# Epilogues of the projections and of the recurrence in more steps, and two evictions on another engine

## The chip, the core and the metric

The kernel runs on one core of a Trainium2 chip. The metric is the device time of one execution in microseconds, from the first to the last instruction and what lies around them. TensorE (PE) does the matmuls, VectorE (DVE), ScalarE (ACT) and GpSimd (POOL) the elementwise work and the copies out of PSUM (evictions), and all large transfers here are queued by SyncE (SP). Each engine takes its own instructions strictly in their order: an instruction that waits holds up all that stand behind it on that engine.

## What is computed

Two blocks of a network over 1024 tokens of width 1024, in fp32 and close to fp32. The first block has an even layer (pooling and a short convolution) and an odd layer, in which the change lies. The odd layer, cut to what matters:

```python
uc, rc, kc, vc, zcc, p1c, p2c, zdc = jnp.split(hc @ in_o[j], 8, axis=-1)      # 256 context tokens
yc_rwkv, ctx_states = rwkv_branch(uc, rc, kc, vc, *rp, None)
u, r, k, v, zc, p1, p2, zd = jnp.split(h @ in_o[j], 8, axis=-1)               # 1024 tokens
y_rwkv, _ = rwkv_branch(u, r, k, v, *rp, ctx_states)
y = odd_merge(y_rwkv, zc, p1, p2, zd, *cp, grid=True)
x = x + gt * y
def rwkv_branch(...):
    r = token_shift_mix(r, mu[0])        # likewise k and v
    g = jax.nn.sigmoid(ugt @ g1) @ g2
    kk = heads(k * k_k); kk = kk / jnp.maximum(jnp.sqrt(jnp.sum(kk * kk, axis=-1, keepdims=True)), 1e-12)
    for d in range(2):                   # two directions; decay, a and k_d come from w1, w2, a1, a2
        s_fin, o = wkv_scan(r_h, heads(decay), k_d, v_h, -kk, kk * a_h, init, reverse=(d == 1))
    o = outs[0] + outs[1]                # normalised per head, times lnx_g, plus lnx_b
    bonus = jnp.sum(r_h * (k_dirs[0] + k_dirs[1]) * r_k, axis=-1, keepdims=True) * v_h
    y = (o + bonus.reshape(b, l, D_BRANCH)) * g
def odd_merge(...):
    y_d = conformer_branch(p1, p2, dw_w, dw_b, ln_g, ln_b, "cols")   # convolution, layernorm, silu
    return jnp.concatenate([y_c * jax.nn.silu(z_c), y_d * jax.nn.silu(z_d)], axis=-1) @ w_out
```

`wkv_scan` is the recurrence: per head a 64x64 state that is decayed, updated and read at each token. The second block (feed-forward, a mixer with sparse attention, feed-forward) is not touched by the change.

## The kernel before

The odd layer is `layer1`. It computes the recurrence in chunks of 64 tokens, four chunks to a group and 40 groups in all: four quarters `i` of the 512 channels, two directions, five groups (one of the context, four of the tokens). A group passes `s1` (decays, the chunk's own products, written to DRAM), `elim` (the triangular inverse on VectorE and GpSimd, once for five groups) and `s2`, which runs nine groups behind `s1`: it makes the local solution KV (evicted on L765), applies the inverse with one set of matmuls whose results go to the two tiles `z[1]` and `z[0]` (evicted on L775, one on ScalarE and one on VectorE), then Q, C, and the states `SI` chunk by chunk.

Beside the recurrence run *dense units*: the input projections of the later quarters (`kvr`), of the conformer (`conf`), of the gate (`zdc`), and last the output projection (`outp`). The main loop adds up a credit per step of the recurrence and pulls dense units from the generator `act` until the units done, `done`, reach it; a unit counts as many as it yields. After each unit `fin(n)` is called. The order of the matmuls of recurrence and dense units on PE is pinned in the order in which they are written; a scheduler at build time places all other instructions, by priority and its own reckoning of when their inputs are there. The epilogues' matmuls are among these.

The *epilogues* are generators in the two lists of `later`: in list 0 the norm of k (`g` in `fk`, then `norm`), the transposes of v, and the layernorm of the conformer (`cln`); in list 1 `finish`, which for each of 16 pieces (quarter `i`, token range `hf`, named 0_3 to 3_0) adds the two directions, forms bonus and gate, normalises and stores. `tick()` takes each list's first generator one step further. In step one a `finish` queues its loads (L814 to L821), adds on GpSimd (L816) and multiplies on VectorE (`KS` in tile `fok`, L822); this step runs when `fin` appends the generator. The next step begins with the matmul BD x KS on PE (L824) and goes to the reciprocal deviation; then come an empty step, the product `dd` on VectorE (L841), and the transposes of `dd` on PE (L844). The `tick` in the same call of `fin` already runs the step with L824. In the k norm, the matmul of the squares `kq` with BO (L523) is in the first step of `g`. The output projection begins when the finishes and layernorms that it reads are done (`fins`), polls for 0.25 of a unit each time, and takes a credit of 4 units ahead of its first matmul.

Of the kernel before, what the change touches and what calls it, by code (L numbers as in the profile page):

```python
# [8 lines left out]
F32=mybir.dt.float32; F32R=mybir.dt.float32r; I32=mybir.dt.int32  # L9
AF=mybir.ActivationFunctionType; ALU=mybir.AluOpType  # L10
# [378 lines left out]
T0,A0,AT,RS0,AR1=0,2,4,5,7  # L389
def bc(ap,shape): return ap.broadcast_to(shape)  # L390
# [88 lines left out]
def layer1(k,I,S,xh,lwd,sgd,gd,x1d,ex):  # L479
# [3 lines left out]
    nc=k.nc; tc=k.tc; V=k.vec; es=ExitStack(); ident=k.ident  # L483
# [8 lines left out]
    BD=P.tile([128,128],F32,name="BD"); nc.gpsimd.memset(BD,0.0)  # L492
    for h in range(2): nc.gpsimd.memset(BD[64*h:64*h+64,64*h:64*h+64],1.0)
    H=[slice(0,64),slice(64,128)]; tg=["f"]
    later=([],[]); fins=set()
    def tick():

        for l in later:
            while l and next(l[0],l) is l: l.pop(0)
    def until(q):  # L500
        while q not in fins:
            if next(later[0][0],later) is later: later[0].pop(0)
# [1 line left out]
    def kvr(i,tags=("f","f","f")):  # L504
# [11 lines left out]
        def fk(c,z,n):  # L516
            t=y3(c); y=t[:,0]; mix(y,z,n,1); nm="%d_%d"%(i,c)
            if c: until(('k',i,c-1))
            q=F.tile([128,256],F32,tag="kq",name="kq"+nm)
            nc.scalar.activation(q,y,AF.Square,scale=V('k_k')[:,i:i+1])  # L520
            def g():
                p=k.ps(tags[2])
                for a in range(2): nc.tensor.matmul(p[:,2*a:2*a+2],q[:,128*a:128*a+128],BO,start=True,stop=True)  # L523
                ss=k.sp.tile([128,4],F32,tag="kss",name="kss"+nm); rn=k.sp.tile([128,4],F32,tag="krn",name="krn"+nm); tm=k.sp.tile([128,4],F32,tag="ktm",name="ktm"+nm)
                nc.vector.tensor_scalar(ss,p[:,:4],1e-30,None,op0=ALU.max)
                g=nc.gpsimd
                g.tensor_tensor(rn,ss,k.mhalf.broadcast_to([128,4]),op=ALU.pow)
                g.tensor_tensor(tm,rn,rn,op=ALU.mult); g.tensor_tensor(tm,tm,ss,op=ALU.mult)
                g.tensor_scalar(tm,tm,-0.5,1.5,op0=ALU.mult,op1=ALU.add); g.tensor_tensor(rn,rn,tm,op=ALU.mult)
                g.tensor_scalar(rn,rn,1e12,1.0,op0=ALU.min,op1=ALU.mult)  # L530
                cur['rn',c]=rn; fins.add(('k',i,c))
                yield
            later[0].append(g())
        def norm(c,m):
            t=y3(c); rn=cur['rn',c]; nm="%d_%d"%(i,c)
            rT=F.tile([2,256],F32,tag="rT",name="rT"+nm)
            p=k.ps(tags[2])
            for a in range(2): nc.tensor.transpose(p[:2,128*a:128*a+128],rn[:,2*a:2*a+2],ident)
            nc.scalar.copy(rT,p[:2,:256])
            yield  # L540
            p=k.ps(tags[2])[:,:256]
            nc.tensor.matmul(p,E2,rT,start=True,stop=True)
            nc.vector.scalar_tensor_tensor(t[:,1],t[:,0],V('k_k')[:,i:i+1],p,op0=ALU.mult,op1=ALU.mult)
            nc.sync.dma_start(KR[:,:m,256*c:256*c+256],t[:,:m]); fins.add(('n',i,c))
            yield
# [26 lines left out]
    def conf(*hb):  # L572

        G=[F.tile([128,1024],F32,tag="big",bufs=2,name="H%d"%hb[0]),S['u'][hb[1]]]; st={}
        def sink(b,c,p):
            cs=slice(256*c-256,256*c); k.n+=1
            while b==0 and c==1 and later[0]: tick()
            if b%2==0: st['sg']=F.tile([128,256],F32,tag="kq",name="sg%d"%k.n); nc.scalar.activation(st['sg'],p,AF.Sigmoid)
            else:
                g=st['sg'] if b//2 else G[0][:,cs]  # L580
                nc.vector.tensor_tensor(g,p,st['sg'],op=ALU.mult)
                if b//2: nc.sync.dma_start(G[1][:,cs],g)
        yield from job(k,I,F,xh,[o+i for i in hb for o in (P20,P10)],range(1,5),sink)
        for g,i in zip(G,hb):
            if i!=hb[0]: g=F.tile([128,1024],F32,tag="big",bufs=2,name="H%d"%i); nc.sync.dma_start(g,G[1])
            acc=F.tile([128,1024],F32,tag="big",bufs=2,name="C%d"%i)
            cw=V('conf_w')[:,31*i:31*i+31]
            nc.vector.tensor_scalar(acc,g,cw[:,15:16],V('conf_b')[:,i:i+1],op0=ALU.mult,op1=ALU.add)
            for a in range(1,16):
                for o in (a,-a):  # L590
                    n=64*(16-a); s0=max(0,64*o); d0=max(0,-64*o)
                    nc.vector.scalar_tensor_tensor(acc[:,d0:d0+n],g[:,s0:s0+n],cw[:,15+o:16+o],acc[:,d0:d0+n],op0=ALU.mult,op1=ALU.add)
            nc.sync.dma_start(S['C'][i],acc)
# [25 lines left out]
    def zdc():  # L619
        n=0  # L620
        for _ in zd():
            yield 1
            n+=1
            if n%4==0 and n>4:
                for t in (n//2-4,n//2-3): later[0].append(cln(t))
        for t in (6,7): later[0].append(cln(t))

    w0h=P.tile([128,8],F32,name="w0h"); a0h=P.tile([128,8],F32,name="a0h"); omka=P.tile([128,4],F32,name="omka")
    nc.vector.tensor_scalar(w0h,V('w0'),0.5,None,op0=ALU.mult); nc.vector.tensor_scalar(a0h,V('a0'),0.5,None,op0=ALU.mult)
# [3 lines left out]
    for d in range(2):  # L633
        m=P.tile([128,2,64],F32,name="MK%d"%d)
# [109 lines left out]
    def s2(u,i,d,g,PC):  # L744
        gm=gmem(d,g); c0=256*gm; isx=gm>0; nm="%d_%d"%(u,g); el=S['el'][u%2]; n=8 if isx else 5
        R=T.tile([128,4,8,64],F32,tag="R2",bufs=2,name="Q"+nm); nc.sync.dma_start(R[:,:,:n],S['rec'][u%4][:,4*g:4*g+4,:n])
# [15 lines left out]
        for c in range(4):  # L762
            for h in range(2): k.pe.matmul(pk[H[h],c],R[H[1-h],c,A0+h],z[h][H[1-h],c,vs],start=True,stop=True)
        for h in range(2): nc.scalar.copy(X[sr(h)],px[sr(h)])
        KV=A0+1; nc.vector.tensor_copy(R[:,:,KV],pk)  # L765
        yield
        for c in range(4):
            for h in range(2): k.pe.matmul(py[fr(h),c],X[sr(h),c],t[sr(h),c,sr(h)],start=True,stop=True)
# [3 lines left out]
        p=k.ps("b1"); p3=p.rearrange("p (a b) -> p a b",a=4)  # L772
        for c in range(4):
            k.pe.matmul(p3[:,c],t[:,c],R[:,c,KV:AT+1].rearrange("p a b -> p (a b)"),start=True,stop=True)
        nc.scalar.copy(z[1][H[1]],p3[H[1]]); nc.vector.tensor_copy(z[0][H[0]],p3[H[0]])  # L775

        m=2 if isx else 1; q=T.tile([128,4,2,64],F32,tag="Q0",name="Q"+nm); C=T.tile([128,4,2,64],F32,tag="Q1",name="C"+nm)
        yield
# [31 lines left out]
    def finish(i,hf):  # L810
# [2 lines left out]
        F2,fb=FP[0]  # L813
        ok=F2.tile([128,4,256],F32,tag="fok",bufs=2,name="fok"+nm); nc.sync.dma_start(ok,S['ok'][i][hf])  # L814
        vv=F2.tile([128,256],F32,tag="fvv",bufs=fb,name="fvv"+nm); nc.sync.dma_start(vv,S['v'][i][:,256*hf:256*hf+256])
        nc.gpsimd.tensor_tensor(ok[:,0:3:2],ok[:,0:3:2],ok[:,1:4:2],op=ALU.add)  # L816
        O,KS=ok[:,0],ok[:,2]
        rz=F2.tile([128,2,256],F32,tag="frz",bufs=fb,name="frz"+nm)
        nc.sync.dma_start(rz[:,0],S['kkr'][i][:,2,256+256*hf:512+256*hf]); nc.sync.dma_start(rz[:,1],S['zc'][i][:,cs])
        sg=F2.tile([96,256],F32,tag="fsg",bufs=fb,name="fsg"+nm); nc.sync.dma_start(sg,sgd[:,cs])  # L820
        g2=F2.tile([96,128],F32,tag="fg2",bufs=fb,name="fg2"+nm); nc.sync.dma_start(g2,I['g2'][:,128*i:128*i+128])  # L821
        nc.vector.scalar_tensor_tensor(KS,KS,V('r_k')[:,i:i+1],rz[:,0],op0=ALU.mult,op1=ALU.mult)  # L822
        yield
        p=k.ps(tg[0]); nc.tensor.matmul(p[:,:256],BD,KS,start=True,stop=True)  # L824
# [14 lines left out]
        yield  # L839
        yield  # L840
        nc.vector.tensor_tensor(dd,dd,bc(rs.unsqueeze(2),[128,4,64]),op=ALU.mult)  # L841
        yield
        p=k.ps(tg[0])
        for t in range(2): nc.tensor.transpose(p[:,128*t:128*t+128],dd[:,2*t:2*t+2].rearrange("p a b -> p (a b)"),ident)  # L844
# [9 lines left out]
    def outp():  # L854
        ed.close()
        xp=ex.enter_context(tc.tile_pool(name="Xp",bufs=1)); X.extend(xt(k,xp,"X") for t in range(8)); X.append(xp)
        with tc.tile_pool(name="op",bufs=1) as P2, k.weights(1,2):
# [9 lines left out]
            for n,(j,bs) in enumerate(((0,(0,1)),(2,(4,5)),(3,(6,7)),(1,(2,)))):  # L867
# [3 lines left out]

                    return lambda r: nc.gpsimd.tensor_tensor(*[a[:,:512*m_].rearrange("p (a b) -> p a b",b=512) for a in (r,r)],gate[:,512*half:512*half+512].unsqueeze(1).broadcast_to([128,m_,512]),op=ALU.mult)
                W=[k.w(I['out_o'][half,j][:,:512*m_],scale=scaled(half)) for half in range(2)]
                yield 0.01+(n==0)*4
                for t in range(8):
                    for half in range(2):
                        p=k.ps("f"); xs=X[t][:,512*half:512*half+512]
# [7 lines left out]
    def fin(n):  # L885
        with tc.high_priority(offset=MPRIO):
            while ready and ready[0][0]<n:
                later[1].append(finish(*ready.pop(0)[1:])); next(later[1][-1])
            tick()
    k.pe=Pinned(tc)  # L890
    N1=40+LAG+1
# [41 lines left out]
    k.pe=nc.tensor  # L933
    while True:
        y=next(act,None); fin(99)
        if y is None and not (ready or later[0] or later[1]): break
    es.close()
    return X[:8],X[8]
ALPHA=float(2**0.25)
# [415 lines left out]
```

## Time and profile before

| | us |
|---|---|
| median of 3 runs | 4145.36 |
| lowest, highest | 4140.95, 4150.91 |
| the profiled execution, its own time | 4132.25 |
| its span, first to last instruction | 4130.5 |

The pipelined part of `layer1` lies between about 690 and 2050 us of the span. In a list of waits, a row says which engine, tile and line waited, for which engine, tile and line, with the total in us, the number of waits and the longest. In a timeline the number in square brackets is the idle time ahead of the instruction, with what ended it. In a table by stretch each row has the stretch, its length, the busy us of the five engines with instructions in brackets, then the granted clock of TensorE as a share of its higher level of 2.4 GHz (0.50 is the lower level, 1.2 GHz), the busy share of the DMA engines, and GB/s.

### The profile page before, as it was taken

The numbers are of one execution on the slowest core, as the hardware profiler recorded it, in microseconds if no ns is written. First come the engines' busy times: TensorE is split into PE (matmuls) and PEld (weight loads), VectorE is DVE, ScalarE is ACT, GpSimd is POOL, SyncE is SP. The second block draws the span as 40 slices with busy tenths as digits, with TensorE's granted clock in tenths as the row PEclk, the third lists the DMA queues.
The fourth block names the chain that finished last, engine by engine and source line by source line (L and its number), as shares of the span: only waits on it lengthen the run. The fifth ranks groups of instructions, "written<-read, shape, count | busy, mean of one in ns | idle before, by whom it ended". The sixth has DMA issues, their size and how long they took to land.

```text
span 4130.5 us, 72373 instructions
## 1 busy us (share of the span) xinstructions
PE 3639.1 (88%) x28552; PEld 3166.6 (77%) x28552; DVE 2384.2 (58%) x4265; ACT 1474.9 (36%) x2581; POOL 1370.3 (33%) x2335
## 2 busy tenths in 40 slices
PE   8999988878786867768679999999999989999997
PEld 6889878767775866646479998876666658999885
DVE  4445331358636635736476665654788666666455
ACT  3233222444432534422232223443565333222333
POOL 3021122246526535624353331111343323333012
PEclk9999999888887887879789999999899999999998
DMA  5453564877675767644322214551231002221554
GB/s 209 154 176 121 166 223 149 258 223 223 212 223 177 225 192 231 188 121 127 112 97 83 84 67 163 179 170 60 75 113 42 21 31 94 78 84 53 205 186 160
DMA packets 422997, 594.52 MB, mean 144 GB/s; under 512 B 106590, under 2 KB 322400, under 8 KB 412928
## 3 DMA queue, kind: packets, MB, share of 16 engines
q1 hardware_dynamic: 422656, 589.88, 44.6%
q8 instruction: 225, 3.69, 0.4%
q14 instruction: 116, 0.95, 0.1%
HBM read 453.45 MB, written 136.07 MB: 143 GB/s over the span
## 4 chain that ended last, share of the span: by engine, by line
PE 58%; DMA 13%; DVE 10%; POOL 6%; issue 6%; ACT 5%; SPq 2%; POOLq 0%; DVEq 0%; ACTq 0%
PE ps L72 13%; PE ps L73 13%; PE ps L74 13%; PE ps L21 10%; DMA wr<-in_f_w 2%; PE ps L1262 2%; PE ps L1250 1%; DVE elUV L738 1%; POOL elTP L737 1%; POOL elUP L738 1%; DVE elTV L737 1%; DMA d_ok<-O 1%; PE ps L1260 1%; DMA raw<-in_in_e 1%; DMA d_xh<-hls 1%
## 5 line engine op out<-in xcount | busy, mean ns | idle before, releaser
L21 PE MATMUL ps<-xq,hi 128*128 128x256 f32 x1632 | 329.4, 302 | 0.0
L72 PE MATMUL ps<-B,ffC 128*128 128x256 f32 x1056 | 298.7, 283 | 5.5 <-DVE ffC L88 2.9
L73 PE MATMUL ps<-B,ffC 128*128 128x256 f32 x1056 | 298.0, 282 | 3.6 <-DVE B L88 3.6
L74 PE MATMUL ps<-B,ffC 128*128 128x256 f32 x1056 | 298.3, 282 | 0.0
L21 PEld LDWEIGHTS ps<-xq,hi 128*128 128x128 f32 x1632 | 280.5, 210 | 3.2 <-issue 2.7
L73 PE MATMUL ps<-w,g 128*128 128x512 f32 x680 | 270.5, 398 | 13.3 <-DVE w L88 12.9
L74 PE MATMUL ps<-w,g 128*128 128x512 f32 x680 | 267.7, 394 | 0.0
L21 PE MATMUL ps<-xq,lo 128*128 128x256 f32 x816 | 258.1, 316 | 1.7 <-DMA xq<-d_xh 1.7
L88 DVE TENSOR_TENSOR w<-wr,w 128x1024 fp32r<-128x1024 f32 x132 | 172.2, 1305 | 138.4 <-ACT w L88 138.0
L72 PE MATMUL ps<-h,lo 128*128 128x320 f32 (+2 forms) x768 | 242.4, 317 | 2.5 <-DVE lo L67 1.7
L73 PE MATMUL ps<-h,hi 128*128 128x320 f32 (+2 forms) x768 | 239.4, 312 | 1.0 <-DVE h L262 1.0
L72 PE MATMUL ps<-w,g 128*128 128x512 f32 x680 | 233.4, 393 | 7.7 <-ACT w L88 4.4
L74 PE MATMUL ps<-h,hi 128*128 128x320 f32 (+2 forms) x768 | 238.9, 311 | 0.0
L67 DVE TENSOR_TENSOR lo<-raw,hi 128x1024 fp32r<-128x1024 f32 (+1 forms) x128 | 159.8, 1249 | 116.1 <-ACT hi L66 115.8
L997 POOL TENSOR_TENSOR ffraw<-ffraw 128x512 f32<-128x512 f32 x44 | 60.1, 1365 | 484.0 <-DVE A L88 484.0
L72 PE MATMUL ps<-B,A 128*128 128x256 f32 x704 | 201.5, 286 | 19.4 <-DVE A L88 18.0
L72 PE MATMUL ps<-B,S 128*128 128x256 f32 x704 | 203.1, 289 | 13.9 <-DVE S L88 13.9
L88 ACT CAST w<-wr 128x1024 fp32r<-128x1024 f32 x132 | 138.6, 1050 | 194.8 <-DMA wr<-in_f_w 111.4
L72 PEld LDWEIGHTS ps<-B,ffC 128*128 128x128 f32 x1056 | 200.0, 189 | 6.4 <-ACT B L88 3.3
L73 PE MATMUL ps<-B,S 128*128 128x256 f32 x704 | 202.6, 288 | 0.2
L73 PEld LDWEIGHTS ps<-B,ffC 128*128 128x128 f32 x1056 | 199.6, 189 | 4.0 <-DVE B L88 4.0
L73 PE MATMUL ps<-B,A 128*128 128x256 f32 x704 | 201.0, 286 | 1.8 <-DVE B L88 1.8
(487 smaller groups left out, 11173.8 us busy)
## 6 DMA issues: line engine op xcount, KB each, us to landing
xq<-d_xh SPq DMA_DIRECT2D x148, 512.0 KB
wr<-in_f_w SPq DMA_DIRECT2D x132, 512.0 KB
ffraw<-in_f_w SPq DMA_DIRECT2D x44, 1024.0 KB
d_rec<-R SPq DMA_DIRECT2D x32, 1024.0 KB
Q<-d_rec SPq DMA_DIRECT2D x32, 1024.0 KB
raw<-in_in_e SPq DMA_DIRECT2D x48, 512.0 KB
d_gg<-ffs SPq DMA_DIRECT2D x88, 256.0 KB
gr<-d_gg SPq DMA_DIRECT2D x44, 384.0 KB
```

The lines of the kernel that those rows point to most:

```text
L21: def matmul(s,*a,**k): return s.pin(s.t.matmul(*a,**k))
L67: nc.vector.tensor_tensor(lo[:,:n],raw[:,:n],hi[:,:n],op=ALU.subtract)
L72: first=t.matmul(ps,lt[1],rt[0],start=start,stop=False)
L73: t.matmul(ps,lt[0],rt[1],start=False,stop=False)
L74: t.matmul(ps,lt[0],rt[0],start=False,stop=stop)
L88: s.nc.scalar.copy(hi,src); s.nc.vector.tensor_tensor(lo,src,hi,op=ALU.subtract)
L737: e.tensor_tensor(t,bc(M[:,sr,x:x+1],[80,ns,nj]),bc(U[:,x:x+1,jr],[80,ns,nj]),op=ALU.mult)
L738: e.tensor_tensor(U[:,sr,jr],U[:,sr,jr],t,op=ALU.add)
L997: nc.gpsimd.tensor_tensor(r[:,1],r[:,1],r[:,0],op=ALU.add)
L1250: p=k.ps("at"); nc.tensor.matmul(p[:,:m],q[r,h//2],kT[r,h//2,c0:c0+m],start=True,stop=True)
L1260: for c in range(m): nc.tensor.transpose(p[:,128*c:128*c+128],s[:,128*(c0+c):128*(c0+c)+128],ident)
L1262: for c in range(b+1): nc.tensor.matmul(po3[r,h//2],VT[:,c,64*h:64*h+64],pT[:,c],start=c==0,stop=c==b)
```

## The change

Five edits, all in `layer1`.

1. `later` has three lists, and `cln` goes to the third. A `tick` advances up to two generators of list 0, and one each of lists 1 and 2; before, it advanced one of each list.
2. The k norm has a step of its own ahead of the BO matmul; `kq` and `rT` get two buffers.
3. `finish` has the loads alone as its first step; the GpSimd add and the VectorE product are the second, the BD matmul opens the third, and there is one more empty step ahead of the transposes. Appending it no longer runs the first step.
4. The credit ahead of the output projection's first matmul goes from 4 to 6 units.
5. KV and both tiles of Z are evicted on ScalarE.

```diff
-    later=([],[]); fins=set()
+    later=([],[],[]); fins=set()
     def tick():
-        for l in later:
-            while l and next(l[0],l) is l: l.pop(0)
+        for l,m in zip(later,(2,1,1)):
+            j=0
+            while j<m and j<len(l):
+                if next(l[j],l) is l: l.pop(j)
+                else: j+=1
...
-            q=F.tile([128,256],F32,tag="kq",name="kq"+nm)
+            q=F.tile([128,256],F32,tag="kq",bufs=2,name="kq"+nm)
             nc.scalar.activation(q,y,AF.Square,scale=V('k_k')[:,i:i+1])
             def g():
+                yield
                 p=k.ps(tags[2])
...
-                for t in (n//2-4,n//2-3): later[0].append(cln(t))
-        for t in (6,7): later[0].append(cln(t))
+                for t in (n//2-4,n//2-3): later[2].append(cln(t))
+        for t in (6,7): later[2].append(cln(t))
...
-        KV=A0+1; nc.vector.tensor_copy(R[:,:,KV],pk)
+        KV=A0+1; nc.scalar.copy(R[:,:,KV],pk)
...
-        nc.scalar.copy(z[1][H[1]],p3[H[1]]); nc.vector.tensor_copy(z[0][H[0]],p3[H[0]])
+        for h in (1,0): nc.scalar.copy(z[h][H[h]],p3[H[h]])
...
-        nc.gpsimd.tensor_tensor(ok[:,0:3:2],ok[:,0:3:2],ok[:,1:4:2],op=ALU.add)
-        O,KS=ok[:,0],ok[:,2]
...
+        yield
+        nc.gpsimd.tensor_tensor(ok[:,0:3:2],ok[:,0:3:2],ok[:,1:4:2],op=ALU.add)
+        O,KS=ok[:,0],ok[:,2]
         nc.vector.scalar_tensor_tensor(KS,KS,V('r_k')[:,i:i+1],rz[:,0],op0=ALU.mult,op1=ALU.mult)
         yield
         p=k.ps(tg[0]); nc.tensor.matmul(p[:,:256],BD,KS,start=True,stop=True)
...
         nc.vector.tensor_tensor(dd,dd,bc(rs.unsqueeze(2),[128,4,64]),op=ALU.mult)
+        yield
         yield
...
-                yield 0.01+(n==0)*4
+                yield 0.01+(n==0)*6
...
-                later[1].append(finish(*ready.pop(0)[1:])); next(later[1][-1])
+                later[1].append(finish(*ready.pop(0)[1:]))
```

The order of instructions differs from that of before in `layer1` alone. Three places follow; an instruction on line L824 of before stands on L829 of after, L523 on L527, L553 on L557, L764 and L765 on L768 and L769, L683 on L687, and L597 on L601.

On PE, the BD matmul of finish 1_1, before. `SI`, `C` and `ident` belong to the recurrence's states, `xq` with `lo` or `hi` to a dense unit, `fok` to the finish:

```order
L21 MATMUL ps_16425<-SI_6197,ident 64x64
L21 MATMUL ps_16425<-C_4_16201,ident 64x64
L824 MATMUL ps_16338<-fok_1_16317,BD 128x256
L826 MATMUL ps_16341<-fsg_1_16325,fg_1_16327 128x256
L829 MATMUL ps_16344<-ident,fok_1_16317 128x128 x2
L21 MATMUL ps_16437<-xq_16439,lo_15496 128x256
```

After:

```order
L21 MATMUL ps_17131<-SI_6197,ident 64x64
L21 MATMUL ps_17131<-C_1_16984,ident 64x64
L21 MATMUL ps_16899<-xq_16900,lo_15507 128x256
L619 MATMUL ps_17169<-ident,cin_16718 128x128 x4
L829 MATMUL ps_17256<-fok_1_17024,BD 128x256
L21 MATMUL ps_16899<-xq_16900,hi_15506 128x256 x2
```

The matmul moved 274 rows back, from the seam ahead of a dense unit into the middle of a later one. Of the twelve finishes from 0_3 to 2_0, the BD matmuls of 0_3, 1_3 and 2_3 moved by 50, 32 and 30 rows, those of 0_2, 1_2 and 2_2 by 102 to 157, and the other six by 274 to 435.

On PE, the norm of k and the transposes of v at the end of the projection of quarter 1 (`kq1_4`, `yv1_4`: chunk 4), before:

```order
L523 MATMUL ps1025_8176<-BO_6155,kq1_3_8139 128x2
L553 MATMUL ps1027_8193<-ident_61,yv1_3_8148 64x64 x8
L523 MATMUL ps1030_8216<-BO_6155,kq1_4_8189 128x2 x2
L21 MATMUL ps1045_8414<-xq1047_8416,lo1035_8393 128x256
L21 MATMUL ps1045_8414<-xq1047_8416,hi1035_8392 128x256 x2
```

After:

```order
L527 MATMUL ps1025_8176<-BO_6155,kq1_3_8139 128x2
L557 MATMUL ps1027_8193<-ident_61,yv1_3_8148 64x64 x8
L557 MATMUL ps1030_8216<-ident_61,yv1_4_8205 64x64 x8
L21 MATMUL ps1045_8413<-xq1047_8415,lo1035_8392 128x256
L527 MATMUL ps1051_8447<-BO_6155,kq1_4_8189 128x2 x2
L21 MATMUL ps1045_8413<-xq1047_8415,hi1035_8391 128x256 x2
```

The BO matmul of 1_4 moved back by a row or two, and the transposes of v that stood eleven rows behind it now stand in its place; chunks 0 to 3 show the same exchange or none.

On ACT, the copies of group 4_1 in `s2`, before (`X` and `TU` are the two steps of the solution, `Pp`, `L`, `BKB` belong to `s1`, `sz` to a dense unit):

```order
L764 COPY X4_1_16404<-ps1644_16739 32x128 x2
L683 ACTIVATE Pp6_1_16709<-L6_1_16707 128x4x64
L683 ACTIVATE L6_1_16707<-L6_1_16707 128x256
L597 ACT_TABLE_LOAD
L597 ACTIVATE sz1646_16792<-ps1623_16437 128x256
```

After:

```order
L768 COPY X4_1_16326<-ps1634_16641 32x128 x2
L769 COPY Q4_1_16312<-ps1634_16641 128x4x64
L687 ACT_TABLE_LOAD
L687 ACTIVATE Pp6_1_16611<-L6_1_16609 128x4x64
L601 ACT_TABLE_LOAD
L601 ACTIVATE sz1636_16694<-ps1614_16359 128x256
```

The copy of KV stands directly behind that of X, and the exponential and the silu of these units alternate, each with its table load; over the whole program ACT has 78 table loads where it had 74.

Ahead of the first matmuls of the output projection, 236 matmuls of the recurrence stood in a row on PE without a dense unit between them, and further back another 144 (56 and 88 around a layernorm); now one stretch of 428 stands there, broken only by epilogues.

## Rows read from the trace of the kernel before

**Rows 1.** The page's first line.

```profile
span 4130.5 us, 72373 instructions
```

**Rows 2.** Table by stretch, layer1: length; PE, PEld, DVE, ACT, POOL busy; clock; DMA; GB/s.

```profile
690.00:2050.00 1360.00, 1030.68 (x12316) 909.65 (x12315) 734.82 (x1741) 513.74 (x1132) 615.75 (x1306) 0.83 0.64 194
```

**Rows 3.** Waits of PE, 700 to 1980 us: us in total, times, longest.

```profile
PE ps L824 <- DVE fok L822: 69.3, 12, 10.5
PE ps L523 <- ACT kq L520: 56.1, 10, 15.7
PE ps L21 <- DVE Z L775: 24.5, 12, 5.9
PE ps L844 <- DVE fd L841: 19.0, 2, 15.7
PE ps L21 <- DVE yo L88: 18.9, 2, 12.6
PE ps L21 <- DVE Q L765: 16.8, 5, 10.0
```

**Rows 4.** Timeline, finishes 1_1 and 1_0: start, duration, engine, line, [idle before].

```profile
1534.04 0.33 SPq L814 DMA_DIRECT2D fok<-d_ok  x1
1538.54 1.26 POOL L816 TENSOR_TENSOR fok<-fok 128x512 f32<-128x512 f32 x1 [1.39 <-DMA fok<-d_ok]
1540.90 0.48 DVE L822 SCALAR_TENSOR_TENSOR fok<-fok,vecs,frz 128x256 f32<-128x256 f32 x1 [0.22 <-issue]
1541.49 1.19 PE L824 MATMUL ps<-fok,BD 128*128 128x256 f32 x2 [10.43 <-DVE fok L822]
1579.95 1.22 PE L824 MATMUL ps<-fok,BD 128*128 128x256 f32 x2 [10.46 <-DVE fok L822]
```

**Rows 5.** Table by stretch, around the wait that ended at 1166.7 us.

```profile
1166.00:1168.00 2.00, 1.32 (x3) 1.14 (x4) 0.54 (x2) 0.00 (x0) 0.11 (x1) 0.50 0.04 12
1168.00:1170.00 2.00, 2.00 (x9) 1.72 (x9) 1.50 (x5) 0.00 (x0) 0.00 (x0) 0.50 0.03 11
```

**Rows 6.** Timeline, first k norms of chunk 4: 0_4, 1_4 whole, 3_4.

```profile
755.15 1.01 PE L523 MATMUL ps<-BO,kq 128*128 128x2 f32 x4 [5.11 <-ACT kq L520]
859.92 0.51 ACT L513 ACTIVATE y<-zk,om 128x256 f32<-128x256 f32 x1 [11.24 <-DMA d_kkr<-y]
861.36 0.51 ACT L520 ACTIVATE kq<-y,vecs 128x256 f32<-128x256 f32 x1 [0.54 <-DVE y L514]
861.92 1.01 PE L523 MATMUL ps<-BO,kq 128*128 128x2 f32 x4 [15.65 <-ACT kq L520]
862.42 0.47 DVE L514 SCALAR_TENSOR_TENSOR yv<-nb,hm,yv 128x256 f32<-128x256 f32 x1
1463.57 1.01 PE L523 MATMUL ps<-BO,kq 128*128 128x2 f32 x4 [12.92 <-ACT kq L520]
```

**Rows 7.** Lines L775 and L765: ns min/median/max, first and last start; the wait on L775.

```profile
L775 ACT COPY Z<-ps x40: 580/580/582, 941.0 to 1992.2; 64x512 f32<-64x512 f32 x40
L775 DVE COPY Z<-ps x40: 669/682/684, 941.8 to 1992.9; 64x512 f32<-64x512 f32 x40
  DVE Z L775: 40.5, 20
L765 DVE COPY Q<-ps x40: 393/410/425, 930.2 to 1989.1; 128x256 f32<-128x256 f32 x40
```

**Rows 8.** Timeline of DVE ahead of a copy of L765.

```profile
1326.25 0.81 DVE L588 TENSOR_SCALAR C<-H,vecs 128x1024 f32<-128x1024 f32 x1 [10.20 <-DMA H<-d_u]
```

**Rows 9.** Groups of ScalarE, 690 to 2050 us: busy, mean ns, idle before.

```profile
L683 ACT ACT_TABLE_LOAD x33 | 42.3, 1283 | 0.6
```

**Rows 10.** Table by stretch: the two stretches ahead of out-projection units.

```profile
1609.00:1661.00 52.00, 33.56 (x462) 29.27 (x460) 18.28 (x45) 20.60 (x47) 19.27 (x43) 0.65 0.90 287
1735.00:1790.00 55.00, 20.05 (x222) 16.18 (x220) 23.90 (x54) 18.89 (x36) 27.03 (x54) 0.59 0.48 124
```

**Rows 11.** Waits of all engines, 660 to 2050 us.

```profile
POOL fok L816 <- DMA fok<-d_ok: 49.2, 12, 8.0
```

More of the change, by code (lines that the diff above doesn't have):

```diff
@@ L535, in norm @@
             t=y3(c); rn=cur['rn',c]; nm="%d_%d"%(i,c)
-            rT=F.tile([2,256],F32,tag="rT",name="rT"+nm)
+            rT=F.tile([2,256],F32,tag="rT",bufs=2,name="rT"+nm)
             p=k.ps(tags[2])
@@ L577, in sink @@
             while b==0 and c==1 and later[0]: tick()
-            if b%2==0: st['sg']=F.tile([128,256],F32,tag="kq",name="sg%d"%k.n); nc.scalar.activation(st['sg'],p,AF.Sigmoid)
+            if b%2==0: st['sg']=F.tile([128,256],F32,tag="kq",bufs=2,name="sg%d"%k.n); nc.scalar.activation(st['sg'],p,AF.Sigmoid)
             else:
@@ L935, in layer1 @@
         y=next(act,None); fin(99)
-        if y is None and not (ready or later[0] or later[1]): break
+        if y is None and not (ready or any(later)): break
     es.close()
```

## The prediction

> **What bounds the kernel now.** I read the page first, for where the change can act: the span is 4130.5 us [rows 1], and the edits lie in `layer1`, from 690 to 2050 us. The table by stretch says what kind of stage that is [rows 2]: in 1360 us PE is busy 1031, DVE 735, ACT 514, GpSimd 616, the DMA engines 0.64 of the time, and TensorE has 0.83 of its higher clock. No engine is full; PE is nearest, and all the others hand it its operands. So the question is what PE, which takes its queue in order, stands and waits for, and that is the next view, the waits of PE [rows 3]. Its largest entries are the places that the change edits: 69.3 us in 12 waits of the finishes' BD matmul for `KS` (L822), 56.1 us in ten waits of the BO matmul for `kq` (L520), 24.5 us in 12 waits for Z (L775), 19.0 us in two waits of the finishes' transposes (L844), 18.9 us in two waits of the output projection for its inputs `yo`, 16.8 us in five for KV (L765).
>
> The timeline shows why the first kind is so long [rows 4]. The load of `fok` for finish 1_1 is queued at 1534.04 us; GpSimd can add at 1538.54, DVE multiplies at 1540.90, and PE, which had nothing else it was allowed to do, starts BD at 1541.49 after 10.43 us of idleness. Load, add and product are a chain of some 7.5 us that lies in the open because BD follows in the same call. A wait has a second price: after the one that ended at 1166.7 us PE ran with a granted clock of 0.50, the level of 1.2 GHz, for its next 1.32 and 2.00 busy us [rows 5], which costs half of 3.3, or 1.7 us.
>
> **The change part by part.** The sum is made against the profiled execution, 4132.25 us; the median of the runs is 13 us above it, and the forecast is moved by that at the end.
>
> *Finish, BD.* Nothing is removed, the matmul is moved: the place in the order shows it 274 rows later for 1_1. PE's pace: between the BD of 1_1 and of 1_0 stood 166 rows, and their starts lie 38.5 us apart, of which 10.5 were idle [rows 4], so 28 us for 166 rows, 6 rows a us. Nine of the twelve finishes move back by 102 to 435 rows, 17 us or more; no wait of this kind was longer than 10.5 [rows 3], so theirs vanish. The first finish of each quarter moves by only 30 to 50 rows, 5 to 8 us, about what load, add and product take; I leave 5 us there in all. Gain 69.3 - 5 = 64 us, and some nine low-clock stretches of 1.7 us, 15 us: 79. The loads, add and product go to other steps too, but none is added; their new neighbours are dense units, which hide them. Without that cover the whole 69 would stay.
>
> *Finish, transposes.* The empty step more gives the reciprocal deviation one more dense unit of time. Of the two waits of 19.0 us the long one, 15.7, had its small GpSimd operations queued behind a piece of `elim`; I take 16 with the clock, between 3 (the short one alone) and 20.
>
> *Norm of k.* Here the profile argues against the edit. At chunk 4 the wait does not come from a matmul that is too early by one unit: ACT could start `y` at 859.92 only when a store had freed the buffer, 11.24 us late, `kq` began at 861.36 and took 0.51, so PE waited 15.65 us [rows 6]. The four waits at chunk 4 (the first, the second and the last are shown) hold 42.7 of the 56.1 us, and the two-buffer tile `y3` is not touched. In the order the transposes of v take the place of BO, and their input `yv` is made right behind, at 862.42 + 0.47 us = 862.89 against 861.87 for `kq`. So PE waits there for `yv` instead, 1.0 us longer. Ten such places would lose 10 us; in some both are ready, and I take a loss of 6. The bounds are a loss of 10 and a gain of 73 (56 and ten times 1.7), if the transposes do not wait.
>
> *Evictions.* DVE copies its Z behind ACT: 0.58 us, then 0.68 [rows 7], since it waits for ACT's half in 20 of 40 groups, 40.5 us in all. After the change ACT makes both, 0.58 + 0.58: on the path 0.1 us less and no handover, some 6 us of the 24.5. For KV the ACT copy costs about as much as the 0.41 us on DVE, but it no longer stands behind what DVE is blocked by, as at 1326 us, where DVE had waited 10.20 us for the load of `H` [rows 8] and PE waited 10.0 for KV. The `SI` products on the same DVE queue are late there too, so I take 9 of the 16.8. Together 15 us. ACT gets 40 x (0.58 + some 0.4) = 39 us and four table loads of 1.28 [rows 9], 44 in all onto 514 busy of 1360, DVE loses 44. The bounds are a loss of 5 (the table loads in the open) and a gain of 41 (all of both waits).
>
> The copies bear on a rule of the Trainium skill. The trace has the two halves of Z one behind the other. The page "PSUM — Partial Sum Buffer", section "PSUM bank collisions raise a hardware error", says that two engines may read one bank at the same time if their partitions lie in different quadrants; ACT's and DVE's halves are such, partitions 64 to 127 and 0 to 63. By it the copies of before could have run side by side, and two on ACT would lose 0.5 us in each of 40 groups, 20 us; the trace does not bear it out here, since the wait of DVE for ACT's copy stands in it.
>
> *Output projection and layernorms.* Before its units the recurrence runs alone, and PE is idle much of the time: 33.6 us busy of 52 in one stretch, 20.1 of 55 in the other, at clocks of 0.65 and 0.59 [rows 10]. By the order these stretches have 236 and 144 matmuls of the recurrence; now there is one of 428. At the first one's pace, 0.22 us each, it lasts 94 us where the two took 107: gain 13. The waits for `yo` (12.6 of the 18.9) are part of the second stretch, and the credit of 6 puts the loads earlier against the matmul. The last finishes, behind the recurrence, move by a few rows; I set them at nothing.
>
> The sum is 79 + 16 - 6 + 15 + 13 = 117 us. Not all of it arrives. While PE stands, the other engines catch up: in each removed gap of up to 10 us DVE, GpSimd and the DMA queue went on with the recurrence, and its next result (Z, KV) will now be waited for a little longer. How much, no row shows; the bounds are nothing and all. I take a third, nearer to nothing than to all, since PE is the busiest engine of the stage with 76% and DVE, the next, has 54% [rows 2]. That leaves 78: 4132 - 78 = 4054 on the profile's scale, **4067 us** as a median. With nothing taken back it is 4028, with two thirds 4106.
>
> **The rivals.**
> *The k waits go as well.* The transposes of v find `yv` ready and BO comes a step later. For it speaks that it is what the edit is written to do at chunks 0 to 3; against it the 11.24 us for a buffer. It adds 79 us, two thirds of which is 53: 4014 us.
>
> *The loads are the bound.* The waits of BD rest on loads: GpSimd waited 49.2 us in 12 cases for `fok` [rows 11], the DMA share was 0.90 in the stretch before the first output units [rows 10]. If transfers set the pace, PE's gaps move to the next operand that comes from DRAM and nothing is won: 4145 us, within 8. Against it: 0.64 over the whole stage, and a chain of load, add and product that simply starts too late.
>
> *The recurrence's own chain is the bound (slower).* Dense units then are cover, not work in the way. A gap removed beside them is found again at Z and KV, and the stretch of 428 matmuls alone goes at the pace of the second stretch, 55 us for 144, 0.38 each: 163 us against 107, a loss of 56. If the other parts kept their two thirds, (117 - 13) x 2/3 = 69, the kernel would still be faster, at 4132; with nothing of them it is 4201. It decides from the point where less than 56 of these 69 arrive; in the middle the time is 4167. Against it: the second stretch is slow for layernorm and `yo` waits that now come elsewhere.
>
> **How the numbers follow.** A difference under 0.2%, 8 us, can hardly be told from none. I give the forecast 0.65, the k rival 0.11, the loads 0.10, the chain 0.14. Faster takes the first two and a little of the last ones (0.03): 0.79. Within 0.2% takes most of the loads, 0.08; slower has the rest, 0.13. The range reaches from 3995, where the k waits go and little is taken back, to 4150, which takes in most of the loads rival and leaves out the chain. Some two in ten lie outside.
>
> **What would show it.** In the waits of PE after, L829 should hold under 15 us before 1980 us; if it holds over 40, the finishes' steps are still too close. L557 should appear with some 40 us for `yv`, with its longest over 12; if it and L527 are both under 20, the k rival is right. Z should have only ACT copies on it, with PE's waits for Z near 18 us. The stretch of the recurrence alone ahead of the first output unit should be near 94 us long; at 160 the chain rival is right. PE's idle time in the stage should be smaller by 60 or more and its clock above 0.85. The prediction is wrong if what PE waits for at R, Z, KV and `SI` grows by as much as L824 loses, or if ACT, with 44 us more, holds up the tanh and exponential of `s1`.

## The result

| | before, us | after, us |
|---|---|---|
| median (4 runs each) | 4145.68 | 4097.50 |
| lowest to highest | 4140.95 to 4150.91 | 4095.07 to 4106.94 |
| span of the profiled execution | 4130.5 | 4093.0 |

The ratio is 0.9888 with a 95% interval from 0.9868 to 0.9907: 1.1% or 48 us faster. The forecast was 78 us faster, 4067.

The whole difference lies in `layer1`. Its stage ends for PE with the first matmul of the next block's feed-forward, here before and, in the second row, after the change, in PE's timeline (start, duration, engine, line, idle before):

```profile
2040.32 0.79 PE L72 MATMUL ps<-B,B 128*128 128x512 f32 x1 [9.86 <-DVE B L88]
...
2001.85 0.79 PE L72 MATMUL ps<-B,B 128*128 128x512 f32 x1 [9.84 <-DVE B L88]
```

That is 38.5 us earlier, and the spans differ by 37.5. Over PE's rows in stretches of 2 us from 692 us to this end, PE's idle time sums to 329 us before and 291 after, 38 less; its busy time is 1020 and 1019. So PE lost waits, and nothing else. The page's first line and the table by stretch answer to [rows 1] and [rows 2]; since the stage is shorter, the stretch holds 48 us of the next block:

```profile
span 4093.0 us, 72359 instructions
```

```profile
690.00:2050.00 1360.00, 1047.59 (x12414) 920.83 (x12414) 736.41 (x1687) 573.84 (x1242) 644.64 (x1351) 0.84 0.65 198
```

ScalarE has 60 us more of work than in [rows 2]; some 20 of them belong to the next block, and up to the stage's end it is 40 (508 before, 548 after), near the 44 of the prediction. TensorE's granted clock is 0.84 where it was 0.83. The waits of PE answer to [rows 3] (us in total, times, longest):

```profile
PE ps L557 <- DVE yv L517: 65.3, 10, 13.3
...
PE ps L542 <- POOL krn L534: 23.7, 3, 16.6
PE ps L21 <- DVE yo L88: 22.9, 3, 16.2
PE ps L21 <- DVE Q L787: 22.4, 6, 8.5
PE ps L829 <- DVE fok L827: 12.1, 6, 3.9
PE ps L21 <- ACT Z L779: 11.9, 12, 3.2
...
PE ps L850 <- DVE fd L846: 7.2, 2, 7.0
...
PE ps L21 <- ACT Q L769: 5.6, 5, 3.8
...
PE ps L829 <- issue: 3.5, 1, 3.5
```

The wait of the finishes for `KS` fell from 69.3 us to 12.1 and 3.5, that of their transposes from 19.0 to 7.2, those for Z and KV from 24.5 and 16.8 to 11.9 and 5.6. Those four lost 89 us. But the k norm's 56.1 us for `kq` are now 65.3 us for `yv`, the norm's transposes wait 23.7 us for the reciprocal norm `krn` (1.2 before), Q's wait for DVE is 22.4 us (6.2 before), and the output projection still waits 22.9. The timeline at chunk 4 of quarter 1 answers to [rows 6]:

```profile
857.13 0.51 ACT L516 ACTIVATE y<-zk,om 128x256 f32<-128x256 f32 x1 [4.78 <-DMA d_kkr<-y]
...
858.19 0.51 ACT L523 ACTIVATE kq<-y,vecs 128x256 f32<-128x256 f32 x1 [0.15 <-DVE y L517]
...
858.65 0.48 DVE L517 SCALAR_TENSOR_TENSOR yv<-nb,hm,yv 128x256 f32<-128x256 f32 x1
...
859.28 1.01 PE L557 MATMUL ps<-ident,yv 64*64 64x64 f32 x14 [13.27 <-DVE yv L517]
```

`kq` ends at 858.70 and PE does not use it; it stands 13.27 us idle for `yv`, ready at 859.13.

### The profile page after: what moved, and what is told of

Its sections match the earlier page's. It is cut to its first block, busy times and chain, and to the rows that moved or that the text cites. A ratio compares the mean times of both kernels' runs of the same rounds, so it can differ in the third digit from the quotient of the medians.

```text
span 4093.0 us, 72359 instructions
## 1 busy us (share of the span) xinstructions
PE 3636.8 (89%) x28552; PEld 3162.4 (77%) x28552; DVE 2352.7 (57%) x4185; ACT 1515.1 (37%) x2665; POOL 1361.8 (33%) x2335
## 4 chain that ended last, share of the span: by engine, by line
PE 56%; DMA 12%; DVE 9%; POOL 8%; issue 7%; ACT 5%; SPq 1%; POOLq 0%; DVEq 0%; ACTq 0%
PE ps L72 13%; PE ps L73 13%; PE ps L74 13%; PE ps L21 9%; DMA wr<-in_f_w 2%; PE ps L1268 2%; PE ps L1256 2%; POOL elUP L742 1%; DVE elTV L741 1%; DVE elUV L742 1%; DMA d_xh<-hls 1%; POOL elTP L741 1%; PE ps L1266 1%; ACT junkA L1158 1%; DMA xq<-d_xh 1%
## 5 line engine op out<-in xcount | busy, mean ns | idle before, releaser
L72 PE MATMUL ps<-B,ffC 128*128 128x256 f32 x1056 | 299.1, 283 | 11.2 <-DVE ffC L88 7.6
```

The costliest lines, as they stand in the source:

```text
L72: first=t.matmul(ps,lt[1],rt[0],start=start,stop=False)
```

## The experiments

Each kernel was timed together with the kernel before on the same chip, in groups; the median of before was 4142.2 us with the first four below, 4139.3 with the next four, 4148.4 with three and 4145.2 with the last. So kernels of different groups are compared by their ratios, and a gain in us is the ratio's, on 4145 us; the distance of two medians can differ from it by a few us. Edits are numbered as in the section on the change.

| kernel | edits on before | ratio | 95% interval |
|---|---|---|---|
| changed kernel | 1 to 5 | 0.9888 | 0.9868 to 0.9907 |
| e1 | 3 | 0.9878 | 0.9856 to 0.9901 |
| e2 | 5 | 0.9955 | 0.9940 to 0.9971 |
| e10 | 3, 5 | 0.9819 | 0.9795 to 0.9843 |
| e20 | 1 (and the buffers) | 1.0048 | 1.0030 to 1.0066 |
| e16 | 3, 5, list for `cln` | 0.9820 | 0.9796 to 0.9845 |
| e13 | 2, 3, 5 | 0.9780 | 0.9755 to 0.9805 |
| e12 | 3, 5, norm queued earlier | 0.9864 | 0.9836 to 0.9892 |
| e3 | changed, without the k step | 0.9884 | 0.9862 to 0.9907 |
| e7 | changed, credit 4 | 0.9893 | 0.9870 to 0.9916 |
| e8 | changed, old evictions | 0.9907 | 0.9886 to 0.9929 |
| e14 | changed, one generator a tick | 0.9818 | 0.9792 to 0.9844 |
| e4 | changed, step ahead of the v transposes | 0.9831 | 0.9809 to 0.9852 |

The theory at the start was the prediction's: epilogue matmuls stand too early in PE's queue, and a later place turns a wait into work. The rival was that the recurrence or the loads set the pace and take back whatever is freed.

**e1, the finish alone.** The diff is that of edit 3 in the section on the change, with the old `tick`.

> The kernel before with edit 3 alone: finish in more steps, the old tick, the old k norm, the old evictions, credit 4. If the finishes' BD matmul only stood too early (theory), its waits fall from 69 us to under 20 and the time by 25 to 45 us, most of the 48 that the whole change brought. If the recurrence's own results or the loads set the pace (rival), the 57 us come back elsewhere and the time stays within 10 us of before. It also tells whether the new wait of the norm's transposes for the reciprocal norm (23.7 us in the changed kernel) belongs to the finishes: theory, it stays near 1 us here.

```profile
PE ps L523 <- ACT kq L520: 54.6, 11, 15.2
...
PE ps L825 <- DVE fok L823: 11.5, 5, 3.4
...
PE ps L846 <- DVE fd L842: 8.9, 2, 7.2
PE ps L21 <- DVE yo L88: 8.0, 3, 4.7
```

Measured: 4093.7 us, ratio 0.9878, 51 us faster (48 between the medians). The wait for `KS` fell to 11.5 us (69.3 in [rows 3]) and the output projection's to 8.0 (18.9). The theory holds, and the 45 us expected at most were a little too few: this edit alone brings as much as all five. A wait for the reciprocal norm is not among its fifteen largest, so that wait does not belong to the finishes.

**e2, the evictions alone.**

```diff
-        KV=A0+1; nc.vector.tensor_copy(R[:,:,KV],pk)
+        KV=A0+1; nc.scalar.copy(R[:,:,KV],pk)
...
-        nc.scalar.copy(z[1][H[1]],p3[H[1]]); nc.vector.tensor_copy(z[0][H[0]],p3[H[0]])
+        for h in (1,0): nc.scalar.copy(z[h][H[h]],p3[H[h]])
```

> The kernel before with edit 5 alone: KV and both halves of Z evicted on ScalarE. Theory: PE's waits for Z and KV fall from 41 us to some 17 as in the changed kernel, of which a half arrives: 5 to 15 us faster. Rival: ScalarE's queue, with 44 us more, holds up s1 and the time is the same or up to 10 us longer.

```profile
PE ps L824 <- DVE fok L822: 65.3, 13, 9.4
...
PE ps L21 <- ACT Z L775: 25.7, 16, 4.0
...
PE ps L21 <- ACT Q L765: 4.2, 5, 1.2
```

Measured: 4128.2 us, ratio 0.9955, 19 us faster (14 between the medians), at the upper end of the expected 5 to 15. The waits for Z and KV were expected to fall to some 17 us and fell to 29.9: in this execution the one for Z did not fall (25.7 us, 24.5 before); the one for KV did, from 16.8 to 4.2. By these rows the gain came mostly from KV, which no longer stands behind blocked work of DVE; no run moves KV alone.

**e3, the changed kernel without the k step.**

```diff
             def g():
-                yield
                 p=k.ps(tags[2])
```

> The changed kernel without the step ahead of the BO matmul (half of edit 2; buffers and lists as changed). Theory: the k and v waits only changed names (BO's 56 us became 65 us of the v transposes), so they become BO's again, some 55 to 65 us in all, and the time stays within 8 us of the changed kernel's 4097. If the step is worth what it was written for, the time rises by 15 us or more.

```profile
PE ps L526 <- ACT kq L523: 57.4, 10, 13.2
...
PE ps L556 <- DVE yv L517: 14.6, 2, 12.4
...
PE ps L541 <- POOL krn L533: 3.2, 3, 2.2
```

Measured: 4097.8 us, ratio 0.9884, the changed kernel's. The wait only has the other name: 57.4 us for `kq` and 14.6 for `yv`, 72 together, where the changed kernel has 65 for `yv`. In company with edit 1 the step is worth nothing. The norm's wait for `krn` is 3.2 us here and 23.7 with the step: with two generators a tick, the step puts BO later and leaves the norm's transposes close behind it (in the changed kernel's longest case BO starts at 1285.53 us, and PE stands at the transposes from 1290.71).

**e8, the changed kernel with the old evictions.** The diff is that of e2, backwards.

> The changed kernel with edit 5 undone: KV and one half of Z back on VectorE. Theory: waits for Z and KV come back to some 35 to 45 us, and 5 to 15 us are lost, 4103 to 4112. If the two copies in a row on ScalarE cost as much as they save, it is within 5 us of 4097. Q's wait for VectorE (22.4 us in the changed kernel, 6.2 before) tells whether that wait came with the evictions or with the finishes.

```profile
PE ps L21 <- DVE Q L787: 10.3, 4, 4.1
```

Measured: 4105.9 us, ratio 0.9907; against 0.9888 that is 8 us slower, as expected, though the two intervals overlap. PE waits 17.4 us for Z and 14.7 for KV, together a little under the 35 to 45 expected, and 10.3 for Q. Of the 16.2 us by which Q's wait had grown (6.2 to 22.4), 12.1 go with the evictions.

**e10, finish and evictions together.** Edits 3 and 5 on the kernel before.

> The kernel before with edits 3 and 5 only (finish in more steps, evictions on ScalarE; old tick, old k norm, credit 4). If the two gains add up, 48 and 16 us, it is at 4078 to 4085, faster than the whole change, and edits 1, 2 and 4 cost some 15 us. If the gains overlap (the second is what the first leaves late), it is at 4088 to 4098, as the changed kernel.

```profile
PE ps L523 <- ACT kq L520: 46.1, 9, 16.0
...
PE ps L21 <- DVE Q L783: 20.8, 7, 6.3
...
PE ps L825 <- DVE fok L823: 11.7, 5, 5.1
```

Measured: 4063.7 us, ratio 0.9819, 75 us faster, more than the 4078 to 4085 us expected. The two gains add up (0.9878 x 0.9955 = 0.9834), and two of the five edits are 28 us faster than all five. From here the question was which of edits 1, 2 and 4 costs so much.

**e7, the credit.**

```diff
-                yield 0.01+(n==0)*6
+                yield 0.01+(n==0)*4
```

> The changed kernel with the output projection's credit back at 4. Theory: the longer stretch of the recurrence alone (428 matmuls in the changed kernel; the order has some 60 rows less with 4) costs more than it saves, so the time falls by 5 to 12 us, to 4086 to 4093. Rival: the credit of 6 covers the loads of yo, PE waits for them longer with 4 (22.9 us in the changed kernel) and the time rises or stays at 4097.

Measured: 4098.4 us, ratio 0.9893, no difference from the changed kernel. The wait for `yo` fell from 22.9 to 9.5 us, but the finishes' BD matmuls waited 21.4 instead of 12.1. My theory, that the credit costs 5 to 12 us, fell.

**e4, the transposes of v a step later as well.**

```diff
             def g():
+                yield
                 p=k.ps(tags[2]); p3=p[:,:256].rearrange("p (a b) -> p a b",a=4)
```

> The changed kernel with a step of its own ahead of the transposes of v too. If the waits at the k and v epilogues (65 us for yv) are a matter of place in PE's queue, as those of the finishes were, they fall under 25 us, and the time by 15 to 35 us. If what bounds them is the arrival of y itself, from the buffer whose store is late, the wait goes to the next instruction that needs it or stays: the time is within 8 us of 4097.

```profile
PE ps L558 <- DVE kss L529: 20.4, 3, 12.1
...
PE ps L542 <- POOL krn L534: 11.4, 6, 6.0
...
PE ps L527 <- ACT kq L523: 7.2, 3, 5.0
```

Measured: 4070.5 us, ratio 0.9831, 24 us faster than the changed kernel. The wait for `yv` is gone; that for `kq` is 7.2 us and that for `krn` 11.4; a part comes back as 20.4 us, in which the transposes of v wait for the PSUM buffer that `kss` frees on DVE. So the k and v waits were a matter of place too, also at chunk 4, where the prediction had put them down to the late buffer: the four waits there were 42.7 us before for `kq` and 40.7 in the changed kernel for `yv`; here a single one over 1 us is left, of 1.4.

**e12, the norm queued earlier**, on e10.

```diff
             if b==2:
                 for q in sh: q.flush()
-                if c==4: fin()
+                fin()
```

> Edits 3 and 5 on the kernel before, and the norm of chunk c queued right behind the projection's R unit, not at the next K unit; the store that frees the buffer for chunk 4 comes some 36 instructions of PE, 6 us, earlier. If the late buffer sets the four waits at chunk 4 (theory), each is 5 us shorter, so 15 to 20 us of PE's wait for kq go against the kernel with edits 3 and 5, and 5 to 15 us of its time. If the waits stay at 50 us or more, the buffer is not what holds them.

```profile
PE ps L523 <- ACT kq L520: 35.0, 11, 6.3
PE ps L21 <- DVE Q L783: 30.7, 7, 7.3
...
PE ps L538 <- POOL krn L530: 11.0, 3, 6.2
```

Measured: 4082.9 us, ratio 0.9864. The buffer does set the four long waits: the longest fell from 16.0 to 6.3 us and the sum from 46.1 to 35.0. The time did not follow; against e10 it rose by some 18 us at the middle of intervals that just overlap. Q waits 30.7 us (20.8 in e10) and the norm's transposes 11.0 for `krn`. The expectation was right on the waits and wrong on the time. These two waits grew by some 20 us where the one for `kq` lost 11; that bringing the norm's matmuls forward is what costs the time fits this and is not shown by itself.

**e13, the k step with the old tick**: edits 2, 3 and 5.

> Edits 2, 3 and 5 on the kernel before: the step ahead of the BO matmul with the old tick, which advances one generator of a list at a time, so that the transposes of v stay behind BO and both come a unit later. Theory: what kept edit 2 from working in the changed kernel is the tick that advances two generators of list 0, which puts the transposes of v in BO's old place; here the waits for kq and yv, 55 us with edits 3 and 5, fall under 25 and the time by 10 to 30 us, to 4035 to 4055. Rival: the wait moves to the reciprocal norm (krn) or the next use of y, and the time stays within 8 us of 4064.

```profile
PE ps L21 <- DMA ld<-d_kkr: 14.8, 1, 14.8
...
PE ps L554 <- DVE kss L526: 12.7, 3, 6.2
...
PE ps L524 <- ACT kq L520: 9.8, 3, 4.6
```

Measured: 4060.1 us beside 4148.4 for before, ratio 0.9780, the fastest of all: 91 us faster than before and 45 faster than the changed kernel. The median lies 5 us above the 4035 to 4055 expected, by the ratio 0.9780 x 4145 = 4054 it lies inside. Against e10 it is 0.4%, with intervals that overlap slightly; beside e16 below, timed in the same group and no different from e10, it is 15 us faster. PE waits 9.8 us for `kq`, and `yv` is not among its nineteen largest waits, where e10 has 46.1 and 8.7; there is 14.8 us for a load of k that the norm stores, and 12.7 for `kss`. The step works where the tick leaves the transposes of v behind BO.

**e14, one generator of each list.**

```diff
-        for l,m in zip(later,(2,1,1)):
+        for l,m in zip(later,(1,1,1)):
```

> The changed kernel with a tick that advances one generator of each list (1, 1, 1 for 2, 1, 1), nothing else. Theory: the second generator is what costs some 30 us, by the wait for yv (65 us) and the one for krn (24 us); without it both fall under 25 together with kq's, and the time by 25 to 45 us, to 4052 to 4072. If the list of its own for the layernorms or the credit is the cost, it stays within 10 us of 4097.

```profile
PE ps L557 <- DVE kss L529: 12.2, 3, 5.0
PE ps L527 <- ACT kq L523: 12.0, 3, 5.4
```

Measured: 4073.0 us, ratio 0.9818, 0.7% or 29 us faster than the changed kernel. One figure in the `tick` does that. The wait for `yv` is gone, the one for `krn` is 3.0 us, and `kq` has 12.0. Against e13, in the same group, the kernel is still 13 us slower, and the two differ by the layernorms' list and the credit alone; the intervals overlap, and no run parts the two there.

**e16, the layernorms in their own list**, on e10 (with `later` of three lists, each advanced by one).

```diff
-                for t in (n//2-4,n//2-3): later[0].append(cln(t))
-        for t in (6,7): later[0].append(cln(t))
+                for t in (n//2-4,n//2-3): later[2].append(cln(t))
+        for t in (6,7): later[2].append(cln(t))
```

> Edits 3 and 5 on the kernel before, and the layernorms in a list of their own (the rest of edit 1 left out: each list advances one generator). Theory: the layernorms only come a little earlier, so the time is within 8 us of edits 3 and 5 alone, 4064. If the list of its own is what costs the changed kernel its 30 us, it is at 4085 or more.

Measured: 4075.5 us beside 4148.4 for before, ratio 0.9820, e10's 0.9819. On edits 3 and 5 the list costs nothing.

**e20, edit 1 alone**: three lists with 2, 1 and 1 generators a tick, on the kernel before, with the second buffer for `kq` and `rT`.

> The kernel before with edit 1 alone (three lists, two generators of list 0 advanced by a tick) and the two buffers each for kq and rT that it needs. Theory: the second generator by itself costs what the changed kernel lacks against edits 3 and 5, so this is 15 to 30 us slower than before, with the waits for kq, yv and krn together over 80 us where before has 66. Rival: it costs only in company with the other edits, and alone the time is within 8 us of before.

```profile
PE ps L526 <- ACT kq L523: 56.1, 11, 12.7
...
PE ps L556 <- DVE yv L517: 15.8, 3, 13.8
PE ps L618 <- DVE cin L614: 14.9, 3, 6.3
```

Measured: 4167.1 us, ratio 1.0048, 20 us slower than before. The waits for `kq` and `yv` are 72 us (56.1 and 8.3, 64 together, before) and the one for `krn` 5.5, so the sum I had put at over 80 came out at 77, and the layernorms' transposes wait 14.9 for their input (3.5 before). These waits are 23 us longer. Up to the stage's end PE's idle time is 14 us longer than before and its busy time 18, in an execution in which 20 us more of busy time are lost to the lower clock. So the cost of edit 1 is shown, and the waits that carry it only in part. Edits 3 and 5 times edit 1 give 0.9819 x 1.0048 = 0.9866; the changed kernel has 0.9888. So its shortfall is edit 1, and by e14 its second generator, except for some 0.2%, within the intervals, that no run assigns.

## Why the prediction was right, and where it was not

*Finish, BD: right.* It said 5 us of the 69.3 would stay; 12.1 stayed, and 3.5 more by another name, 15.6 in all beside its mark of 15. e1 shows that edit 3 alone, transposes included, is worth 51 us.

*Finish, transposes: not borne out.* 19.0 us fell to 7.2, and in e1 to 8.9, but they are 18.0 in e10, 21.2 in e13 and 15.9 in e14, in more and shorter waits. The one long wait of 15.7 us is gone in all of them; the sum comes and goes with the schedule, and the 7.2 of the changed kernel are in part luck.

*Evictions: right.* 15 us were put down; e2 gives 19, undoing them in the changed kernel 8. PE's waits for Z and KV sum to 17.5, the prediction's mark was 18 for Z alone, which has 11.9. That ScalarE would hold up `s1` did not come true. In e2 Z's share was overrated and KV's underrated: Z's wait stayed, KV's lost 12.6 us, the 9 assumed were too few. That two engines might copy the halves side by side, as the page "PSUM — Partial Sum Buffer" of the Trainium skill has it for different quadrants (section "PSUM bank collisions raise a hardware error"), no run here tried. The wait of DVE for ACT's copy in [rows 7] shows that the program ran them one behind the other, not whether the chip had to. With both on one engine PE's wait for Z is 25.7 us in e2, no shorter than the 24.5 of before.

*Output projection: the stretch came out shorter, and bought nothing.* The prediction's two stretches of 52 and 55 us [rows 10] hold output units as well: by PE's timeline before, the units stop at 1609.75 and 1722.93, and matmuls on `yo` follow at 1653.75 and 1775.22, so the recurrence ran alone for 44.0 and 52.3 us, 96 together.

```profile
1609.35 0.40 PE L21 MATMUL ps<-xq,hi 128*128 128x256 f32 x2
...
1653.75 0.79 PE L21 MATMUL ps<-hi,yo 128*128 128x512 f32 x1
...
1722.54 0.39 PE L21 MATMUL ps<-hi,yo 128*128 128x512 f32 x1
...
1775.22 0.78 PE L21 MATMUL ps<-hi,yo 128*128 128x512 f32 x1
```

After, the one stretch runs from the end of the last `xq` matmul to the first on `yo`, 77 us where 94 were worked out:

```profile
1581.44 0.40 PE L21 MATMUL ps<-xq,hi 128*128 128x256 f32 x2
...
1658.84 0.48 PE L21 MATMUL ps<-hi,yo 128*128 128x512 f32 x1
...
1675.94 0.79 PE L21 MATMUL ps<-hi,yo 128*128 128x512 f32 x1 [16.16 <-DVE yo L88]
```

It is 19 us shorter than the two before, where the prediction put down 13. Behind the first three matmuls of the unit PE then waits 16.16 us for `yo`, which the credit of 6 was to cover (12.58 before). The credit does not make the stretch either: with 4 in e7 it is 77.4 us long, the wait for `yo` is shorter and the time the same.

*Norm of k: the step that failed.* The prediction saw in the order that the transposes of v take BO's place, and set that at a loss of 6 us, with bounds of -10 and +73. The exchange itself it had right: the wait kept its size under a new name, where it would have needed both matmuls later. What it missed is that the tick with two generators, which causes the exchange, is a loss by itself: it sends the transposes of v into the same unit as BO, and the norm's transposes into the unit right behind. e20 measures edit 1 alone at 20 us slower, e14 the second generator at 29 us in company, where it also keeps the k step from paying. With 6 us put down for it, the term was mis-sized by 14 to 23 us. The rival "the k waits go as well" was written off for the late buffer; e13 and e4 show that a place later on PE is enough, since nothing on PE has to stand still while the buffer comes free: at chunk 4 the four waits of 42.7 us are 5.8 in e13, counting those over 1 us.

*The third taken back: the number fits, in part by luck.* e10 has edits 3 and 5, so neither the k term nor the output projection's; without these the prediction's sum was 79 + 16 + 15 = 110 us, two thirds of it 73. e10 gained 75, with an interval of 65 to 85. But the third was a choice between nothing and all. In e10's trace, one execution as each trace is, the four edited waits lost 88 us and PE's idle time up to the stage's end 76, so an eighth was taken back, while two terms of the sum did not come: the transposes' 16, of which 1 is left there, and the low-clock price. In the changed kernel the four waits lost 89 us, as much, and PE's idle time 38: the 38 us between the two kernels are edits 1, 2 and 4 and not the recurrence catching up, and e14, with 84 us less idle time than before, puts them on the second generator.

The low-clock price, 15 us for nine stretches, cannot be found. Busy time lost to the lower clock (busy times one less the granted clock, summed over the 2-us stretches) is 131 us before and 120 after, but 134 in e10, which gained more, and 140 in e1, where PE's idle time fell by 58 us and its busy time grew by 15. The marks of a clock above 0.85 and of 60 us less idle time were missed, with 0.84 and 38.

*The rivals.* The loads did not set the pace: GpSimd waited longer for `fok` after than before (58.8 us in 12 cases, 49.2 in [rows 11]) and PE's wait fell by 57, or 54 with the 3.5 us by another name. The recurrence's own chain did not either: the stretch alone kept the fast pace, Z and KV lost 24 us of PE's waits, and R and `SI` gained 10 (25.8 to 31.7 and 7.3 to 11.2).

## What to carry to other kernels

Where an engine takes its queue in order, an operand's wait is removed by putting independent work ahead of the instruction, and this must be done for each instruction that reads what comes out of the same chain: the k step paid nothing until the transposes of v went back with it. A helper that advances several epilogues at a time moves instructions forward again; measure it by itself. When a change has several parts, try them alone: here two of five gave 75 us, the five together 48, and three of them 91.

## What the hardware showed

The 16.6-us wait for `krn` has a cause that I had not looked for. In the changed kernel's timeline DVE had stood 11.98 us for the load of `H`, so that `kss` came late and GpSimd stood 8.49 us of the wait for it. Then DVE worked through the conformer's convolution, and the small GpSimd operations on 128x4 elements ran beside it; the first row below is such an operation on another tile while DVE still stood:

```profile
1290.36 0.20 POOL L84 TENSOR_SCALAR rst<-rst 128x4 f32<-128x4 f32 x1
...
1298.26 0.81 DVE L592 TENSOR_SCALAR C<-H,vecs 128x1024 f32<-128x1024 f32 x1 [11.98 <-DMA H<-d_u]
...
1299.34 2.37 POOL L531 TENSOR_TENSOR krn<-kss,mhalf 128x4 f32<-128x4 f32 x1 [8.49 <-DVE kss L529]
...
1305.03 1.04 POOL L533 TENSOR_TENSOR krn<-krn,ktm 128x4 f32<-128x4 f32 x1
...
1306.05 1.08 DVE L596 SCALAR_TENSOR_TENSOR C<-H,vecs,C 128x832 f32<-128x832 f32 x1
1306.16 1.07 POOL L534 TENSOR_SCALAR krn<-krn 128x4 f32<-128x4 f32 x1
...
1307.28 0.59 PE L542 MATMUL ps<-ident,krn 128*2 128x128 f32 x2 [16.57 <-POOL krn L534]
```

The last two GpSimd operations took 1.04 and 1.07 us beside DVE operations of 1.08, and ended with them. The last of the six takes a quarter of that in the median: the rows of its line over the stage (ns, min/median/max) are

```profile
L534 POOL TENSOR_SCALAR krn<-krn x20: 232/247/1096, 685.8 to 1451.3; 128x4 f32<-128x4 f32 x20
```

So six small operations, the first at 2.37 us (1.04 in the median of its line), became 7.9 us of chain, the other half of the wait. Of the GpSimd operations on 128x4 elements in this stage other than that first kind, 127 started while DVE ran nothing; their median is 0.20 us and the longest took 0.26. That the two engines share something which DVE holds during its instruction fits these rows. The Trainium skill has such a rule (page "GPSIMD Engine Reference", section "1. Specifications"): GpSimd shares its way to SBUF with VectorE, and DVE instructions with two inputs in SBUF contend with it, as this one has, which reads H and C. No run here took the convolution away to test it.
